# Two projections of a hybrid decoder: q and k computed channel by channel, and rotated by way of a DMA

## The chip, the cores and the metric

The kernel runs on one core of a Trainium2 chip. The metric is the device time of one execution in microseconds (us).

The engines are named as in the profile: PE multiplies matrices, PEld loads its weights, DVE, ACT and POOL work on vectors, SP issues most DMAs. Each engine works through its own queue in order. L537 is line 537 of the kernel; in the changed kernel the same line stands some ten to twenty lines further down.

## The reference

Two decoder layers on one sequence of 512 tokens, 1024 wide. Per layer, the normalised input is projected to ten groups of 512 columns, and four mixers work on them:

```
h    = rms_norm(x, g);  proj = h @ w_in           # 1024 -> 10 * 512
a_u, a_g, q, k, v, b_g, c_x, c_g, m_q, m_g = split(proj)
y_a  = s5_mixer(a_u)                              # state space, GLU
y_b  = rms_norm(diff_attention(rope(q), rope(k), v))
y_c  = rglru_mixer(c_x)                           # conv, gates, scan over time
y_m  = memory_attention(m_q, rms_norm(mem) @ w_mem_kv)
x   += concat(y_a*silu(a_g), y_b*silu(b_g), y_c*silu(c_g), y_m*silu(m_g)) @ w_out
```

q and k have 4 heads of 2 times 64 channels. `rope` rotates channels 0 to 15 of every 64: `x1*cos - x2*sin` and `x2*cos + x1*sin`, where x1 is channels 0 to 7, x2 is 8 to 15, and the angle depends on token and channel. Everything is float32.

## The kernel before, in words

**Split products.** Every weight comes by DMA in pieces of 128x1024 (`raw`). ACT casts a piece to `whi` (L166) and DVE subtracts to get the rest, `wlo` (L172). The input is split in the same way (hThi, hTlo). Each product is three matmuls: high by high, high by low, low by high.

**Two forms of a projection.** `tm_block` (L524) has the tokens as weights and gives token by channel, in four accumulators at once; its matmuls are L537. `cm_block` (L504) has the weight piece as weights and gives channel by token, in two accumulators, two calls for 512 columns; its matmuls are L517. There are four accumulators (`acc`) in PSUM in all.

**The order.** `ORDER` (L31) is the sequence of projections of each layer. `kv` stands for the memory's keys (`mk`, two calls of `cm_block`, 256 wide, four weight pieces) and values (`mv`, `tm_block` with two accumulators, four pieces). In layer 1 of before the sequence begins q, k, cx, v, kv.

**The streams.** Everything else runs beside the projections: attention (L610), the recurrent unit `lru` (L724, started when cx is finished), S5, the memory's norm. Each is a generator that is stepped at ticks, one per twelve matmuls of a projection. Attention has 16 items a layer (four token tiles by four heads): scores (L647, L648, L650) by PE, a maximum on DVE, exponentials on ACT (L658), a weighted difference on DVE, transposes on PE (L672), the product with v (L682), and two passes of ACT over it (L683, L685). A scheduler then orders the instructions of each engine by the program order and its own estimates, and where a buffer has to come free first, by that.

**lru.** Four channel blocks: a cast (L735), two products with small matrices `bd` (L740 to L742), two tanh on ACT (L743), a second tanh (L748), exponentials (L751), squares (L753), one root over 128x2048 (L756), and then on DVE a product with the root (`xc<-xc,li`) and a scan over time (L760). Only behind its last scan come its buffers free.

**Buffers.** `b8` tiles (128x2048) share 14 places. The result of mk and mv is a pair of them, `kv` high and low: ACT writes the high part (L796), DVE the low part (`kv<-acc,kv`), and with the latter the accumulator comes free.

**q and k.** Both are `tm_block`. `qk_evac` (L574) copies an accumulator to `qz` and rotates it by four DVE instructions; `flush_qk` (L591), called at each tick, transposes four 128x128 blocks on PE (L597) and copies them to `qT`, or splits them into the two `kT`.

Of the kernel before, what the change touches and what calls it, by code (L numbers as in the profile page):

```python
# [17 lines left out]
P = 128  # L18
# [9 lines left out]
ROPE_THETA = 500000.0  # L28


ORDER = ["q v k kv cx au cg bg mq ag mg gl oAM0 oAM1 oBC0 oBC1".split(),  # L31
         "q k cx v kv au mq bg mg ag cg gl oAM0 oAM1 oBC0 oBC1".split()]

C_ID, C_DM, C_IF, C_KEEP, C_CM, C_END = 0, 128, 144, 152, 152, 280

# [13 lines left out]


MEM_AHEAD = 2
BD_AHEAD = 3
S5P_AT = 2
D_MEM = (3, 2, 1)
D_S5 = (1, 1, 2, 2, 1, 2)
D_AT = 2


class Streams:
# [31 lines left out]
def tile_kernel(ctx: ExitStack, tc: tile.TileContext, A, out):  # L91
# [17 lines left out]
    def b8(shape, name, dtype=F32):  # L109
        return big.tile(shape, dtype, tag="b8", name=nm(name))  # L110
# [4 lines left out]
    def b2(shape, name, dtype=F32):  # L115
        return sm2.tile(shape, dtype, tag="b2", name=nm(name))
# [10 lines left out]
    def tp(shape=(P, 4, 128)):  # L127
        return ps.tile(list(shape), F32, tag="tp", bufs=2, name=nm("tp"))
# [51 lines left out]


    xr = A["x"].rearrange("o (t p) d -> p (o t) d", p=P)
    xd = ctx.enter_context(tc.tile_pool(name="xd", bufs=1, space=bass.MemoryType.DRAM)).tile([L, D], F32, tag="xd", name="xd")
    xdr = xd.rearrange("(t p) d -> p t d", p=P)
    xt = {}

# [32 lines left out]
    for l in range(DEPTH):  # L219
        for n in ORDER[l]:  # L220
            if n == "kv":
                for u in range(2):
                    add(l, "mk", u, cm_pieces(A["w_mem_kv"][l], 256 * u))
                add(l, "mv", 0, tm_pieces(A["w_mem_kv"][l], 512))
            elif n == "gl":
                w = A["s5_w_glu"][l].rearrange("(k p) (s c) -> p k s c", p=P, s=2)
                for u in range(2):
                    add(l, "gl", u, [w[:, 2 * i:2 * i + 2, :, 256 * u:256 * u + 256] for i in range(2)])
            elif n[0] == "o":
                ps_ = []  # L230
                for g in n[1:3]:
                    r0 = 512 * "ABCM".index(g)
                    ps_ += tm_pieces(w_out[l, r0:r0 + 512], 512 * int(n[3]))
                add(l, "o", n[1:], ps_)
            elif n in ("q", "k", "v", "au"):
                add(l, n, 0, tm_pieces(w_in[l], COL[n]))
            else:
                for u in range(2):
                    add(l, n, u, cm_pieces(w_in[l], COL[n] + 256 * u))
# [106 lines left out]
    def tt(o, a, b, op):  # L346
        V.tensor_tensor(out=o, in0=a, in1=b, op=op)  # L347
# [136 lines left out]
        V.tensor_scalar(out=cpos, in0=cpos, scalar1=4.0, scalar2=None, op0=ALU.mult)  # L484


    idb = const.tile([P, P], BF16, tag="idb", name="idb")
    cmb = const.tile([P, P], BF16, tag="cmb", name="cmb")
    V.tensor_copy(idb, ident)
# [81 lines left out]
        return ((lambda k, t: hi[k // 4][:, k % 4, t, :]), (lambda k, t: lo[k // 4][:, k % 4, t, :]))  # L571


    def qk_evac(dst):  # L574
        def f(t, a):
            z = b2([P, 8, 64], "qz")
            S.copy(z, a.rearrange("p (m d) -> p m d", d=64))
            z12 = z[:, :, 0:16].rearrange("p m (s f) -> p m s f", f=8)
            ca = rcos[:, t, :].unsqueeze(1).unsqueeze(1).to_broadcast([P, 8, 2, 8])
            sa = rsin[:, t, :].unsqueeze(1).unsqueeze(1).to_broadcast([P, 8, 2, 8])  # L580
            rab = b2([P, 2, 8, 2, 8], "rab")
            ra, rb = rab[:, 0], rab[:, 1]
            tt(ra, z12, ca, ALU.mult)
            tt(rb, z12, sa, ALU.mult)
            tt(z12[:, :, 0, :], ra[:, :, 0, :], rb[:, :, 1, :], ALU.subtract)
            tt(z12[:, :, 1, :], ra[:, :, 1, :], rb[:, :, 0, :], ALU.add)
            pend.append((dst, t, z, st.now))
        return f

    pend = []  # L590
    def flush_qk():  # L591

        while pend and st.now - pend[0][3] >= 2:
            dst, t, z, _ = pend.pop(0)
            pt = tp()
            for j in range(4):
                PE.transpose(pt[:, j, :], z[:, 2 * j:2 * j + 2, :].rearrange("p m d -> p (m d)"), ident)  # L597
            ts = slice(t * 128, (t + 1) * 128)
            if len(dst) == 1:
                S.copy(dst[0][:, :, ts], pt)  # L600
            else:

                for m in range(2):
                    own, oth = slice(m * 64, m * 64 + 64), slice(64 - m * 64, 128 - m * 64)
                    S.copy(dst[m][own, :, ts], pt[own])
                    tt(dst[m][oth, :, ts], pt[own], dst[m][own, :, ts], ALU.subtract)

    st.hook = flush_qk

    def attention(l, R):  # L610
        while pend or "par" in st.live:
            yield
        qT, kT, v = R["qT"][0], R["kT"], R["v"]
        o = qT
        R["o"] = o
        oss = const.tile([P, 16], F32, tag="oss", name=nm("oss"))
# [499 lines left out]
    def run(gen):  # L1116
        for _ in gen:
            st.tick()
# [36 lines left out]
    for pi, (l, n, u, ids) in enumerate(plan):  # L1155
# [6 lines left out]
        if any(p[0] == l and p[1] == "cx" for p in plan[pi:pi + BD_AHEAD]) and "bd" not in R:  # L1162
            lru_load(l, R)
        if n in ("q", "k"):
            R[n + "T"] = [b8([P, 4, L], "qT")] if n == "q" else [b8([P, 4, L], "kT", F32R) for _ in range(2)]
            run(tm_block(h_tm(), qk_evac(R[n + "T"]), ids))
        elif n == "v":
            vt = R["v"] = b8([P, NT, 512], "v")

# [78 lines left out]
        elif n == "gl":  # L1248
# [4 lines left out]
            for hf, pid in enumerate(ids):  # L1253
                whi, wlo = (w.rearrange("p (k s c) -> p k s c", k=2, s=2) for w in w_use(pid))
                for j in range(2):
# [13 lines left out]
                        ag = R["ag"][:, 2 * u + j, :]  # L1269
                        V.scalar_tensor_tensor(out=ag, in0=th, scalar=0.25, in1=ag, op0=ALU.mult, op1=ALU.mult)  # L1270
                    st.tick()
        if n in ("q", "k", "v") and all(a in R for a in ("qT", "kT", "v")):
            st.start("attn", attention(l, R))
        if n == "o":
            pair, half = u[:2], int(u[2])
# [99 lines left out]
```

## Time and profile before

| | us |
|---|---|
| median of three runs | 913.9 (913.62 to 914.91) |
| the profiled execution | 913.18 |
| its span | 911.4 |
| PE busy | 890.5 |
| DVE busy | 658.8 |
| ACT busy | 509.6 |

The busy time of PE comes from modelled ends: a matmul of 512 columns is shown as about 0.39 us long, and the next begins 0.23 us after it. So two starts are compared where a matmul's cost is wanted, and not the length of one.

### The profile page before, as it was taken

To read this page: it belongs to the slowest core of one execution; us is meant where nothing else is said; L and a number is where in the kernel's file an instruction comes from. 1 tells how busy PE (TensorE), PEld (TensorE's weight loads), DVE (VectorE), ACT (ScalarE), POOL (GpSimd) and SP (SyncE) were. 2 spreads that over 40 slices of the span, in tenths; PEclk is the share of its full clock that TensorE was granted. 3 is DMA by queue.
4 is the path that set the end of the run, shared out by engine and by line. 5 is a ranking of instruction groups with operands and counts; after the bars stand their busy time and mean duration, and the time that the engine had idled before them with its cause. 6 is when DMAs were issued, how large, how long until landed. Compare 5 with 4: busy or idle time off the path is not lost.

```text
span 911.4 us, 12490 instructions
## 1 busy us (share of the span) xinstructions
PE 890.5 (98%) x4542; PEld 748.9 (82%) x4542; DVE 658.8 (72%) x1315; ACT 509.6 (56%) x1031; POOL 42.1 (5%) x86
## 2 busy tenths in 40 slices
PE   8999999999999999999999999999999999999996
PEld 5788888978878888888888888898888888788885
DVE  6985888678999856983474667764899996666343
ACT  6764887985434265922554568766655344863133
POOL 1001000001110100000100000000101110000000
PEclk9999999999999999999999999999999999999999
DMA  5733432212222237432343332432112222152322
GB/s 185 196 118 102 140 93 70 70 47 72 75 70 61 75 104 205 135 111 93 127 140 92 93 93 70 137 95 70 51 47 83 63 74 93 47 185 98 108 72 93
DMA packets 80930, 90.07 MB, mean 99 GB/s; under 512 B 23778, under 2 KB 58211, under 8 KB 80868
## 3 DMA queue, kind: packets, MB, share of 16 engines
q1 hardware_dynamic: 77842, 85.72, 30.3%
q10 hardware_dynamic: 722, 2.36, 0.8%
q0 software_dynamic: 2304, 1.18, 0.5%
q8 instruction: 36, 0.59, 0.3%
q14 instruction: 26, 0.21, 0.1%
HBM read 84.40 MB, written 4.19 MB: 97 GB/s over the span
## 4 chain that ended last, share of the span: by engine, by line
PE 72%; DVE 18%; ACT 6%; issue 2%; DMA 1%; SPq 0%; DVEq 0%; ACTq 0%
PE acc L537 37%; PE acc L517 17%; PE acc L1261 5%; DVE wlo L172 2%; DVE u L347 2%; DVE xr L1046 2%; DVE wt L347 2%; PE ms L682 1%; DVE xr L347 1%; PE tp L312 1%; PE sc L810 1%; PE tp L1012 1%; PE sc L647 1%; PE sc L648 1%; ACT whi L166 1%
## 5 line engine op out<-in xcount | busy, mean ns | idle before, releaser
L172 DVE TENSOR_TENSOR wlo<-raw,whi 128x1024 fp32r<-128x1024 f32 x136 | 166.2, 1222 | 125.3 <-ACT whi L166 121.6
L166 ACT CAST whi<-raw 128x1024 fp32r<-128x1024 f32 x136 | 143.1, 1052 | 194.1 <-PE acc L537 120.1
L517 PE MATMUL acc<-hThi,whi 128*128 128x512 f32 x384 | 154.3, 402 | 0.0
L517 PE MATMUL acc<-hThi,wlo 128*128 128x512 f32 x384 | 151.1, 394 | 0.0
L517 PE MATMUL acc<-hTlo,whi 128*128 128x512 f32 x384 | 150.6, 392 | 0.0
L537 PE MATMUL acc<-whi,hThi 128*128 128x512 f32 x256 | 104.1, 407 | 1.0 <-ACT whi L166 1.0
L537 PE MATMUL acc<-wlo,hThi 128*128 128x512 f32 x256 | 100.7, 393 | 0.0
L537 PE MATMUL acc<-whi,hTlo 128*128 128x512 f32 x256 | 100.7, 394 | 0.0
L537 PE MATMUL acc<-wlo,mxh 128*128 128x512 f32 x256 | 100.2, 391 | 0.0
L537 PE MATMUL acc<-whi,mxh 128*128 128x512 f32 x256 | 100.1, 391 | 0.0
L537 PE MATMUL acc<-whi,mxl 128*128 128x512 f32 x256 | 100.1, 391 | 0.0
L517 PEld LDWEIGHTS acc<-hThi,wlo 128*128 128x128 f32 x384 | 72.2, 188 | 15.0
L517 PEld LDWEIGHTS acc<-hTlo,whi 128*128 128x128 f32 x384 | 72.4, 189 | 13.4
L517 PEld LDWEIGHTS acc<-hThi,whi 128*128 128x128 f32 x384 | 72.4, 189 | 13.0
L537 PEld LDWEIGHTS acc<-whi,hThi 128*128 128x128 f32 x256 | 56.3, 220 | 9.1 <-ACT whi L166 1.4
L537 PEld LDWEIGHTS acc<-whi,hTlo 128*128 128x128 f32 x256 | 56.1, 219 | 7.8 <-DVE hTlo L315 0.2
L537 PEld LDWEIGHTS acc<-wlo,hThi 128*128 128x128 f32 x256 | 56.4, 220 | 7.1
L537 PEld LDWEIGHTS acc<-whi,mxl 128*128 128x128 f32 x256 | 48.1, 188 | 9.8
L537 PEld LDWEIGHTS acc<-wlo,mxh 128*128 128x128 f32 x256 | 48.1, 188 | 9.7
L537 PEld LDWEIGHTS acc<-whi,mxh 128*128 128x128 f32 x256 | 48.1, 188 | 9.6
L982 POOL DMA_DIRECT2D MT<-kq x64 | 32.1, 509 | 490.7 <-DVE kq L347 339.4
L658 ACT ACTIVATE e<-sc,nmx 128x128 f32<-128x128 f32 (+3 forms) x64 | 33.1, 524 | 7.1 <-DVE nmx L654 5.8
(316 smaller groups left out, 1642.2 us busy)
## 6 DMA issues: line engine op xcount, KB each, us to landing
raw<-in_w_in_dram SPq DMA_DIRECT2D x80, 512.0 KB, 3.7
raw<-in_w_out_dram SPq DMA_DIRECT2D x32, 512.0 KB, 3.3
raw<-in_w_mem_kv_dram SPq DMA_DIRECT2D x16, 512.0 KB, 3.3
x<-in_x_dram SPq DMA_DIRECT2D x8, 512.0 KB, 4.7
raw<-in_s_w_glu_dram SPq DMA_DIRECT2D x16, 256.0 KB, 3.1
mt<-in_mem_dram SPq DMA_DIRECT2D x4, 512.0 KB
xd<-x SPq DMA_DIRECT2D x4, 512.0 KB, 4.0
x<-xd SPq DMA_DIRECT2D x4, 512.0 KB, 5.6
```

The costliest lines, as they stand in the source:

```text
L166: S.copy(hi, wbuf[j])
L172: V.tensor_tensor(out=lo, in0=raw, in1=hi, op=ALU.subtract)
L312: lastins["pe"] = PE.transpose(pt[:, k, :], h[:, kk * 128:(kk + 1) * 128], ident)
L347: V.tensor_tensor(out=o, in0=a, in1=b, op=op)
L517: PE.matmul(a[j][:, :ncol], w[:, kk, c], h(k), start=(hf == 0 and i == 0), stop=(hf == 1 and i == 3 * nh - 1))
L537: PE.matmul(a[t], h(k, t), w[:, kk, :], start=(p == 0 and kk == 0 and i == 0), stop=(p == np_ - 1 and kk == 1 and i == 2))
L647: PE.matmul(s[:, m, :M], qh[:, m, h, :], kT[m][:, h, :M], start=True, stop=False)
L648: PE.matmul(s[:, m, :M], ql[:, m, h, :], kT[m][:, h, :M], start=False, stop=False)
L658: S.activation(e[:, m, :N], s[:, m, :N], AF.Exp, bias=nmx[:, m:m + 1], scale=0.125, accum_out=sm[:, m:m + 1])
L982: G.dma_start(out=MT[g * 64 + 64 - n:g * 64 + 64, g, t], in_=kq[g * 64:g * 64 + n])
L1046: V.tensor_tensor_scan(out=xr_[i][:, j, :], data0=dec, data1=xr_[i][:, j, :], initial=0.0, op0=ALU.mult, op1=ALU.add)
L1261: PE.matmul(a, w[:, k, s, j * 128:(j + 1) * 128], h[:, 2 * hf + k, :], start=(hf == 0 and i == 0), stop=(hf == 1 and i == 5))
```

## The change

v comes first in both layers. q and k become `cm_block`, so their channels stand on the partitions, and attention takes its q straight from that tile (`qz`). To rotate, `rope` copies the 16 rows of every 64 that are to be rotated to a tile of their own with four POOL DMAs, computes with four DVE instructions, and writes them back with four DMAs. k is then split into the two `kT` with four ACT casts and four DVE subtractions of 64x1024. The cosines and sines that this needs, channel by token, are made once at the start: eight POOL copies, eight transposes on PE, four ACT copies; they are kept in DRAM for layer 1. Attention waits for both `rope` streams. `BD_AHEAD` goes from 3 to 1, which loads the small matrices of `lru` just before cx. By count, 64 transposes of q and k go and 8 come, ACT has 12 instructions fewer and DVE 56 fewer; the number of projection matmuls is the same.

```diff
@@ -28,8 +28,8 @@
 ROPE_THETA = 500000.0
 
-ORDER = ["q v k kv cx au cg bg mq ag mg gl oAM0 oAM1 oBC0 oBC1".split(),
-         "q k cx v kv au mq bg mg ag cg gl oAM0 oAM1 oBC0 oBC1".split()]
+ORDER = ["v q k kv cx au cg bg mq ag mg gl oAM0 oAM1 oBC0 oBC1".split(),
+         "v q k cx kv au mq bg mg ag cg gl oAM0 oAM1 oBC0 oBC1".split()]
 
 C_ID, C_DM, C_IF, C_KEEP, C_CM, C_END = 0, 128, 144, 152, 152, 280
 
@@ -49,11 +49,12 @@
 
 MEM_AHEAD = 2
-BD_AHEAD = 3
+BD_AHEAD = 1
 S5P_AT = 2
 D_MEM = (3, 2, 1)
 D_S5 = (1, 1, 2, 2, 1, 2)
 D_AT = 2
+D_ROPE = {"q": ((2, 2), (2, 2)), "k": ((4, 4), (2, 2))}
 
 class Streams:
@@ -232,7 +234,7 @@
                     r0 = 512 * "ABCM".index(g)
                     ps_ += tm_pieces(w_out[l, r0:r0 + 512], 512 * int(n[3]))
                 add(l, "o", n[1:], ps_)
-            elif n in ("q", "k", "v", "au"):
+            elif n in ("v", "au"):
                 add(l, n, 0, tm_pieces(w_in[l], COL[n]))
             else:
                 for u in range(2):
@@ -484,6 +486,23 @@
         V.tensor_scalar(out=cpos, in0=cpos, scalar1=4.0, scalar2=None, op0=ALU.mult)
 
+
+
+    rtab = [b2([P, L], f"rt{i}") for i in range(2)]
+    rtd = [dpool.tile([P, L], F32, tag=f"rtd{i}", name=f"rtd{i}") for i in range(2)]
+    for w, src in enumerate((rcos, rsin)):
+        rep_ = b2([P, NT, P], "rep")
+        for i in range(NT):
+            G.tensor_copy(rep_[:, i].rearrange("p (a f c) -> p a f c", a=4, c=4),
+                          src[:, i].unsqueeze(1).unsqueeze(3).to_broadcast([P, 4, 8, 4]))
+        pr = tp()
+        for i in range(NT):
+            PE.transpose(pr[:, i, :], rep_[:, i], ident)
+        pf = pr.rearrange("p i c -> p (i c)")
+        for s_ in range(2):
+            S.activation(rtab[w][s_ * 64:s_ * 64 + 64], pf[s_ * 64:s_ * 64 + 64], AF.Copy, scale=-1.0 if w == 1 and s_ == 1 else 1.0)
+        G.dma_start(out=rtd[w], in_=rtab[w])
+
     idb = const.tile([P, P], BF16, tag="idb", name="idb")
     cmb = const.tile([P, P], BF16, tag="cmb", name="cmb")
     V.tensor_copy(idb, ident)
@@ -571,46 +590,44 @@
         return ((lambda k, t: hi[k // 4][:, k % 4, t, :]), (lambda k, t: lo[k // 4][:, k % 4, t, :]))
 
-    def qk_evac(dst):
-        def f(t, a):
-            z = b2([P, 8, 64], "qz")
-            S.copy(z, a.rearrange("p (m d) -> p m d", d=64))
-            z12 = z[:, :, 0:16].rearrange("p m (s f) -> p m s f", f=8)
-            ca = rcos[:, t, :].unsqueeze(1).unsqueeze(1).to_broadcast([P, 8, 2, 8])
-            sa = rsin[:, t, :].unsqueeze(1).unsqueeze(1).to_broadcast([P, 8, 2, 8])
-            rab = b2([P, 2, 8, 2, 8], "rab")
-            ra, rb = rab[:, 0], rab[:, 1]
-            tt(ra, z12, ca, ALU.mult)
-            tt(rb, z12, sa, ALU.mult)
-            tt(z12[:, :, 0, :], ra[:, :, 0, :], rb[:, :, 1, :], ALU.subtract)
-            tt(z12[:, :, 1, :], ra[:, :, 1, :], rb[:, :, 0, :], ALU.add)
-            pend.append((dst, t, z, st.now))
-        return f
-
-    pend = []
-    def flush_qk():
-
-        while pend and st.now - pend[0][3] >= 2:
-            dst, t, z, _ = pend.pop(0)
-            pt = tp()
-            for j in range(4):
-                PE.transpose(pt[:, j, :], z[:, 2 * j:2 * j + 2, :].rearrange("p m d -> p (m d)"), ident)
-            ts = slice(t * 128, (t + 1) * 128)
-            if len(dst) == 1:
-                S.copy(dst[0][:, :, ts], pt)
-            else:
-
+    def rope(l, R, n):
+
+
+        z = R[n + "z"]
+        if l and n == "q":
+            rtab[:] = [b2([P, L], f"rt{i}") for i in range(2)]
+            for w in range(2):
+                G.dma_start(out=rtab[w], in_=rtd[w])
+        x1, x2 = b2([P, L], "rx"), b2([P, L], "ry")
+        rows = [(x1[s_ * 64 + m * 32:s_ * 64 + m * 32 + 32], z[m * 64 + s_ * 8:m * 64 + s_ * 8 + 8])
+                for s_ in range(2) for m in range(2)]
+        for x_, z_ in rows:
+            G.dma_start(out=x_, in_=z_)
+        yield D_ROPE[n][l][0]
+        co, si = rtab
+        for s_ in range(2):
+            to, fr = slice(s_ * 64, s_ * 64 + 64), slice(64 - s_ * 64, 128 - s_ * 64)
+            tt(x2[to], x1[fr], si[fr], ALU.mult)
+        tt(x1, x1, co, ALU.mult)
+        tt(x1, x1, x2, ALU.add)
+        for x_, z_ in rows:
+            G.dma_start(out=z_, in_=x_)
+        yield D_ROPE[n][l][1]
+        if n == "k":
+
+            kT = R["kT"] = [b8([P, 4, L], "kT", F32R) for _ in range(2)]
+            for h in range(0, 4, 2):
+                hs = slice(h, h + 2)
                 for m in range(2):
                     own, oth = slice(m * 64, m * 64 + 64), slice(64 - m * 64, 128 - m * 64)
-                    S.copy(dst[m][own, :, ts], pt[own])
-                    tt(dst[m][oth, :, ts], pt[own], dst[m][own, :, ts], ALU.subtract)
-
-    st.hook = flush_qk
+                    S.copy(kT[m][own, hs], z[own, hs])
+                    tt(kT[m][oth, hs], z[own, hs], kT[m][own, hs], ALU.subtract)
+                yield
 
     def attention(l, R):
-        while pend or "par" in st.live:
+        while any(n in st.live for n in ("par", "ropeq", "ropek")):
             yield
-        qT, kT, v = R["qT"][0], R["kT"], R["v"]
+        qT, kT, v = R["qz"], R["kT"], R["v"]
         o = qT
         R["o"] = o
         oss = const.tile([P, 16], F32, tag="oss", name=nm("oss"))
@@ -1162,8 +1179,15 @@
         if any(p[0] == l and p[1] == "cx" for p in plan[pi:pi + BD_AHEAD]) and "bd" not in R:
             lru_load(l, R)
         if n in ("q", "k"):
-            R[n + "T"] = [b8([P, 4, L], "qT")] if n == "q" else [b8([P, 4, L], "kT", F32R) for _ in range(2)]
-            run(tm_block(h_tm(), qk_evac(R[n + "T"]), ids))
+            if u == 0:
+                R[n + "z"] = b8([P, 4, L], n + "z")
+            zt = R[n + "z"]
+
+            def z_evac(j, a, u=u, zt=zt):
+                S.copy(zt[:, 2 * u + j, :], a)
+            run(cm_block(h_cm(), 8, z_evac, ids))
+            if u == 1:
+                st.start("rope" + n, rope(l, R, n))
         elif n == "v":
             vt = R["v"] = b8([P, NT, 512], "v")
 
@@ -1269,7 +1293,7 @@
                         ag = R["ag"][:, 2 * u + j, :]
                         V.scalar_tensor_tensor(out=ag, in0=th, scalar=0.25, in1=ag, op0=ALU.mult, op1=ALU.mult)
                     st.tick()
-        if n in ("q", "k", "v") and all(a in R for a in ("qT", "kT", "v")):
+        if n == "k" and u == 1:
             st.start("attn", attention(l, R))
         if n == "o":
             pair, half = u[:2], int(u[2])
```

The next rows are the order of DVE in layer 1 of before, at the end of `lru`. `wlo` is the low part of a weight piece, `mx` the maximum of an attention item.

```order
L347 TENSOR_TENSOR xc_4938<-xc_4938,li_5129 128x512 x2
L172 TENSOR_TENSOR wlo_5304<-raw_5192,whi_5302 128x1024
L760 SCALAR_TENSOR_TENSOR li_5129<-lr_5128,xc_4938 128x512 x2
L347 TENSOR_TENSOR xc_4938<-xc_4938,li_5129 128x512
L172 TENSOR_TENSOR wlo_5350<-raw_5264,whi_5348 128x1024
L652 TENSOR_REDUCE mx_5388<-sc_5371 128x2
L760 SCALAR_TENSOR_TENSOR li_5129<-lr_5128,xc_4938 128x512
L654 TENSOR_SCALAR nmx_5390<-mx_5388 128x2
L347 TENSOR_TENSOR xc_4938<-xc_4938,li_5129 128x512
L172 TENSOR_TENSOR wlo_5416<-raw_5306,whi_5414 128x1024
L760 SCALAR_TENSOR_TENSOR li_5129<-lr_5128,xc_4938 128x512
```

The same place on DVE in the changed kernel; L777 is the scan, `kv_5190` the low part of mk, and acc_5191 to acc_5369 are the four accumulators of mk.

```order
L771 SCALAR_TENSOR_TENSOR li_5236<-a_1032_5573,li_5236 128x512
L671 TENSOR_SCALAR nmx_5622<-mx_5620 128x2
L349 TENSOR_TENSOR xc_4953<-xc_4953,li_5236 128x512 x2
L777 SCALAR_TENSOR_TENSOR li_5236<-lr_5235,xc_4953 128x512 x2
L349 TENSOR_TENSOR xc_4953<-xc_4953,li_5236 128x512
...
L777 SCALAR_TENSOR_TENSOR li_5236<-lr_5235,xc_4953 128x512 x2
L349 TENSOR_TENSOR kv_5190<-acc_5191,kv_5189 128x256
L349 TENSOR_TENSOR kv_5190<-acc_5192,kv_5189 128x256
L349 TENSOR_TENSOR kv_5190<-acc_5368,kv_5189 128x256
L349 TENSOR_TENSOR kv_5190<-acc_5369,kv_5189 128x256
```

Before, weight pieces were split between the scans, and the accumulators of mk were emptied one by one later on. Now all four stand full until the last scan, and are emptied behind it in one go.

PE in the changed kernel, from the last matmul of mk to the first of mv (`acc_5522`); `sc` are scores of attention items.

```order
L536 MATMUL acc_5369<-mhi_5086,wlo_5279 128x256
L664 MATMUL sc_5461<-kT_5062,qh_5462 128x256
...
L664 MATMUL sc_5542<-kT_5062,qh_5462 128x256
...
L664 MATMUL sc_5613<-kT_5062,qh_5462 128x256
...
L664 MATMUL sc_5693<-kT_5062,qh_5462 128x256
...
L699 MATMUL ms_5718<-v_4532,pT_5636 128x128 x2
L556 MATMUL acc_5522<-whi_5370,mhi_5086 128x512
```

And PE in before, at the same step of the sequence.

```order
L517 MATMUL acc_5477<-mlo_5173,whi_5414 128x256
L517 MATMUL acc_5477<-mhi_5172,wlo_5416 128x256
L537 MATMUL acc_5604<-whi_5478,mhi_5172 128x512
L672 MATMUL tp_5581<-cst,e_5509 128x128
L682 MATMUL ms_5585<-v_5105,pT_5520 128x128
L537 MATMUL acc_5604<-wlo_5480,mhi_5172 128x512
```

In before mv followed mk at once. Now four attention items stand between the two, with no matmul of a projection among them.

PE early in layer 0 of the changed kernel, in the first projection (now v); `rep` is what POOL writes for the tables.

```order
L556 MATMUL acc_355<-whi_357,hThi_128 128x512
L500 MATMUL tp_301<-cst,rep_296 128x128 x4
L556 MATMUL acc_355<-wlo_359,hThi_128 128x512
L556 MATMUL acc_355<-whi_357,hTlo_130 128x512
L556 MATMUL acc_356<-whi_357,hThi_128 128x512
```

In before only projection matmuls stood here; the transposes of the tables are new on PE.

## Rows read from the trace of the kernel before

**Rows 1.** The page, parts 1 and 2: busy time, then forty slices of the span.
```profile
PE 890.5 (98%) x4542; PEld 748.9 (82%) x4542; DVE 658.8 (72%) x1315; ACT 509.6 (56%) x1031; POOL 42.1 (5%) x86
PE   8999999999999999999999999999999999999996
```
**Rows 2.** Busy time by window: stretch, its length, engines, granted clock, DMA share.
```profile
160.00:200.00 40.00, 40.00 (x210) 35.47 (x210) 26.18 (x42) 34.96 (x68) 0.00 (x0) 1.00 0.21 66
240.00:280.00 40.00, 38.53 (x213) 32.64 (x213) 39.33 (x71) 15.88 (x35) 8.01 (x16) 1.00 0.28 84
533.00:564.00 31.00, 31.00 (x150) 25.60 (x149) 21.22 (x29) 28.92 (x42) 0.00 (x0) 1.00 0.18 58
560.00:600.00 40.00, 39.06 (x243) 34.79 (x243) 33.17 (x63) 28.15 (x74) 0.00 (x0) 1.00 0.43 131
```
**Rows 3.** Timeline of PE around eight transposes of q: start, length, instruction.
```profile
42.43 0.39 PE L537 MATMUL acc<-whi,hTlo 128*128 128x512 f32 x1
42.66 1.03 PE L597 MATMUL tp<-cst,qz 128*128 128x128 f32 x8
43.45 0.47 PE L537 MATMUL acc<-whi,hThi 128*128 128x512 f32 x1
43.76 0.39 PE L537 MATMUL acc<-wlo,hThi 128*128 128x512 f32 x1
```
**Rows 4.** Groups by line and shape, PE: busy, mean ns, idle before, releasers.
```profile
L597 PE MATMUL tp<-cst,qz 128*128 128x128 f32 x64 | 8.9, 274 | 2.0 <-DVE tA L347 1.3 <-DVE kT L347 0.4 <-DVE rden L347 0.3
```
**Rows 5.** Timeline of PE early in layer 0.
```profile
29.51 0.39 PE L537 MATMUL acc<-whi,hThi 128*128 128x512 f32 x1
```
**Rows 6.** Timeline of DVE there: the last step of the cosines.
```profile
30.06 0.19 DVE L393 TENSOR_SCALAR cs<-cs 128x64 f32<-128x64 f32 x1
```
**Rows 7.** Groups by line and shape, POOL.
```profile
L1133 POOL DMA_DIRECT2D bd<-in_lru_w_a_dram x4 | 2.6, 663 | 0.0
...
L1129 POOL MEMSET bd<- 128x512 f32 x4 | 2.1, 526 | 212.8 <-issue 105.6 <-DVE sn L917 59.5 <-PE tp L891 26.6
```
**Rows 8.** Issues of DMAs: count, size, median us to landing.
```profile
bd<-in_lru_w_x_dram POOLq DMA_DIRECT2D x4, 64.0 KB, 3.2
```
**Rows 9.** Timeline of ACT in layer 1, from cx's last evacuation to the root.
```profile
534.29 0.58 ACT L1181 COPY cx<-acc 128x512 f32<-128x512 f32 x1
...
557.94 1.92 ACT L756 ACTIVATE li<-li 128x2048 f32<-128x2048 f32 x1
559.76 1.03 ACT L166 CAST whi<-raw 128x1024 fp32r<-128x1024 f32 x1
```
**Rows 10.** Timeline of DVE behind the root.
```profile
559.89 1.29 DVE L347 TENSOR_TENSOR xc<-xc,li 128x512 f32<-128x512 f32 x2 [2.54 <-ACT li L756]
...
562.24 2.33 DVE L760 TENSOR_TENSOR_SCAN li<-lr,xc 128x512 f32<-128x512 f32 x2
```
**Rows 11.** Timeline of ACT for one attention item.
```profile
575.50 0.36 ACT L658 ACTIVATE e<-sc,nmx 128x128 f32<-128x128 f32 x1
...
576.20 0.26 ACT L674 COPY pT<-tp 128x128 f32<-128x128 f32 x1
576.34 0.38 ACT L683 ACTIVATE qT<-ms,rc 128x128 f32<-128x128 f32 x1
...
576.95 0.39 ACT L796 CAST kv<-acc 128x256 fp32r<-128x256 f32 x1
```
**Rows 12.** Groups by line and shape, ACT.
```profile
L631 ACT CAST qh<-qT 64x512 fp32r<-64x512 f32 x16 | 9.9, 619 | 0.2
...
L605 ACT CAST kT<-tp 64x512 fp32r<-64x512 f32 x16 | 8.8, 581 | 2.8 <-PE tp L597 2.4
```
**Rows 13.** Timeline of PE in mk: one matmul, one attention item.
```profile
573.29 0.28 PE L517 MATMUL acc<-mhi,wlo 128*128 128x256 f32 x1
573.41 0.28 PE L647 MATMUL sc<-kT,qh 128*128 128x256 f32 x1
...
573.98 0.36 PE L517 MATMUL acc<-mhi,whi 128*128 128x256 f32 x1
```

More of the change, by code (lines that the diff above doesn't have):

```diff
@@ L182, in tile_kernel @@
     xr = A["x"].rearrange("o (t p) d -> p (o t) d", p=P)
-    xd = ctx.enter_context(tc.tile_pool(name="xd", bufs=1, space=bass.MemoryType.DRAM)).tile([L, D], F32, tag="xd", name="xd")
+    dpool = ctx.enter_context(tc.tile_pool(name="xd", bufs=1, space=bass.MemoryType.DRAM))
+    xd = dpool.tile([L, D], F32, tag="xd", name="xd")
     xdr = xd.rearrange("(t p) d -> p t d", p=P)
```

## The prediction

> **What bounds the kernel now.** I read the busy times first: PE is busy in 98% of the span, and in nearly every slice [rows 1]. So a change is worth what it takes from PE's queue, or what it makes PE wait. The second view is the busy time by window, for how near the other two engines are to their own limit: in 160 to 200 us ACT is busy 34.96 of 40 us, in 240 to 280 DVE 39.33 of 40, in 533 to 564 ACT 28.92 of 31 [rows 2]. In the last of these PE still never waits. The third view is the timeline, since a busy PE there is only two starts apart: matmuls of 512 columns begin 0.23 us apart [rows 3], of 256 columns 0.12 us [rows 13].
>
> All sums are made in the profiled execution (913.18 us, span 911.4); the median of the runs is 0.7 us above it, which I add at the end.
>
> **The transposes.** Eight of them stand between starts at 42.66 and 43.45, and the matmul behind them takes 0.31 us to its successor in place of 0.23 [rows 3]: 0.79 + 0.08 = 0.87 us, 0.109 each. 64 go and 8 come: -56 x 0.109 = -6.1 us. The projection matmuls stay in number and width, so they cost the same. PE waits 2.0 us in all in front of those transposes, 1.3 of it once, for DVE [rows 4]: -2.0. What is late next there is nothing on PE's path, since q's tile is needed only by attention.
> The Trainium skill, "TensorE: Matmul & The Clock Gate", Part 4 on the PE-mode transpose, gives about 275 ns for one transpose of 128x128 in a kernel's context. The trace agrees on the length (274 ns [rows 4]), but a length is not a cost here: by it 56 would be worth 15.4 us, an estimate that the starts contradict.
>
> **The tables at the start.** In the changed order the first transposes of the tables stand where PE is at about 29.6 us, one matmul after [rows 5]. The cosines end at 30.06 + 0.19 = 30.25 [rows 6], and then POOL makes four copies of 128x128. No such copy is in the trace; a memset of 128x512 takes 0.526 us [rows 7], so four copies take 0.5 us if they go by elements and 2.1 us if each costs as much as that memset. PE then waits until 30.8 to 32.4: 1.1 to 2.7 us, and I take 2.0. The second table's copies run under the six matmuls and the transposes behind the first; 0 to 0.4 us, taken as nothing. Everything behind the transposes in PE's queue is late by the same 2.0, since PE has no slack.
>
> **The rotation by DMA.** POOL issues four copies out and four back, 0.66 us each [rows 7], of 64 KB; the nearest transfer of this size lands after 3.2 us [rows 8]. So 2.6 + 3.2 = 5.8 us from the first issue to the last landing, against two ticks of 24 matmuls, 24 x 0.23 = 5.5 us. DVE may wait 0.3 us for each trip, with a weight piece queued behind. Between that and twice as much (a first landing that takes as long as the issues) it is 0 to 1.5 us on DVE; PE gets nothing of it as long as the pieces are made several us ahead. I take 0. POOL itself has 5% of the span to do [rows 1]. ACT and DVE instructions that go or come are hidden under PE, except in the two places that follow.
>
> **Layer 1 from cx to mv.** This is the term that decides. Before, v came between cx and kv: 96 x 0.23 = 22 us of PE work beside which `lru` ran. Now mk follows cx at once. In the changed order DVE empties the four accumulators of mk only behind the last scan of `lru`, and mv, which needs these accumulators, stands behind that on PE. So I compare when that scan ends with how much PE has to do until then, both from the end of cx (T0).
> ACT: in before the root over 128x2048 ended 557.94 + 1.92 = 559.86, and cx's last copy began at 534.29 [rows 9]: 25.6 us, with ACT 93% busy. In the changed order, the same stretch of ACT's queue has in addition two casts of weights (2 x 1.03 [rows 9] = 2.1), four casts of k of 64x1024 (512 elements take 0.58 [rows 12], 1024 in a weight's cast 1.03: between 2.3 and 4.6, I take 4.1), four casts of mk (4 x 0.39 [rows 11] = 1.6), the exponentials of six items (575.50 to 576.20 is 0.70 an item [rows 11], two of them wider by about 0.2: 4.6), six copies of transposed items (0.14 to 0.3: 1.2), four pairs behind the product with v (576.34 to 576.95, 0.61 each [rows 11]: 2.4), and four casts of q (4 x 0.62 [rows 12] = 2.5). Together 18.5, so 44.1 us to the end of the root if ACT waits no more than before.
> DVE behind the root: two products 1.2 us to the next start and two scans 2.33 [rows 10], so four of each 7.1, small instructions of attention about 0.9, and the first emptied accumulator 0.4. mv begins at T0 + 52.5.
> PE until then: 96 matmuls of 256 columns x 0.12 = 11.5; 24 products of `lru` x 0.23 = 5.5; scores of eight items, 573.41 to 573.98 [rows 13], x 0.57 = 4.6; 26 transposes and 8 products with v x 0.11 = 3.7. Together 25.3. So PE waits 27 us if ACT waits no more than it did.
> It will wait more: each item goes from PE to DVE to ACT and back, and one tile of scores is there at a time. At the 87% of 160 to 200 us in place of 93%, 44.1 becomes 47.2 and the wait 30; reckoned as work that ACT fills to 87% it is 50.7 and 34. I take 32. The low end is 25 (k's casts at 0.58), the high end 46: the 70% share of ACT in 560 to 600 [rows 2], where attention, mk and weights ran together, makes 44.1 into 63.
>
> **Attention later in layer 0.** It starts when k is rotated, so some six items more fall into S5's stretch, with about 1.7 us of DVE each, 10 us, where DVE is busy 39.33 of 40 and PE loses 1.5 already [rows 2]. Weight pieces are made up to some pieces ahead, so most is swallowed: 0 to 5, I take 1.5.
>
> **Small waits in kv.** In 560 to 600 PE lost 0.94 us [rows 2] by attention beside mk; these go into the long wait: -1.
>
> **Sum.** -6.1 - 2.0 + 2.0 + 32 + 1.5 - 1 = +26.4: 939.6 in the profiled execution, 940 by the median.
>
> **Rivals.**
> 1. The other side, faster: mk's accumulators come free in time. The point from which it decides is whether the last scan ends before PE has done its 25.3 us behind cx. Then only -6.1 - 2.0 + 2.0 + 0.5 - 0 is left, 908. For it speaks that PE never waited in 533 to 564 [rows 2]; against it that the same chain took 25.6 us to the root alone, without attention, and 7 us of products and scans come behind it. Chance 0.06, with a spread of 905 to 911.
> 2. Only `lru`'s own chain counts, since attention's and k's ACT work (18.5 us) comes earlier or later than the order suggests, as it would if the rotations landed late: 25.6 + 8.4 - 25.3 leaves a wait of 9, so 940 - 23 = 917. Chance 0.08, spread 914 to 924.
> 3. S5's stretch in layer 0 is the second loss: DVE is full there, and 10 us more work is 10 us more time beyond what is swallowed, on top of the forecast: 948. For it speaks the 39.33 of 40 [rows 2], against it that other stretches around have room. Chance 0.12.
> 4. PE's clock. The granted clock is 1.00 in all windows read, also in 533 to 564 [rows 2], but in before PE is never thin for long. If PE, doing 25 us of work in nearly 60, came down to the lower level of 1.2 GHz, its work would be hidden in the wait, but scores in the chain of an item and the first matmuls behind would take twice their 0.23: some ten matmuls and four items, 3 to 5 us more, 944. Chance 0.12.
> The Trainium skill, "TensorE: Matmul & The Clock Gate", Part 1 on the HAM clock gate, says that an array that was idle falls to 1.2 GHz and has to be warmed by work; no stretch of before shows it on a long wait.
>
> The forecast itself, a long wait in layer 1 and the rest small, has 0.62: 930 to 953. The 80% range is 924 to 954: it leaves out rival 1, most of rival 2, and the far end of the waits. What a measurement of this kernel can tell from no change is about 0.2%, 1.8 us: faster 0.06, the same 0.03 (the low end of rival 2), slower 0.91.
>
> **What would show it.** In the profile after: two or three slices of PE well below 9 in the middle of the span, and there ACT above 85%; the longest wait of PE by far in front of the first matmul of mv, put down to a DVE `kv` instruction, with all scans before it; the root ending 44 to 51 us after cx's last copy. Small: a wait of 1 to 3 us at about 30 us for POOL's `rep`, none for q's transposes. I am wrong if PE stays full in layer 1 (rival 1), if the root comes some 26 us after cx (rival 2), or if PE thins out at 200 to 320 us (rival 3).

## The result: 4% slower, and the profile after

The changed kernel takes 949.7 us (948.2 to 951.2) against 913.8; the ratio is 1.0389 (95% interval 1.0373 to 1.0405). The forecast was 940, between 924 and 954. The profiled execution took 949.12 us with a span of 947.3, 35.9 us more than before.

Parts 1 and 2 of the page, as in [rows 1], with the granted clock:

```profile
PE 897.8 (95%) x4486; PEld 750.6 (79%) x4486; DVE 656.3 (69%) x1259; ACT 506.4 (53%) x1019; POOL 64.7 (7%) x130
...
PE   7999799999999999999999969389999999999997
...
PEclk9999999999999999999999989589999999999999
```

Only POOL has clearly more to do, 64.7 us in place of 42.1, and PE is shown 7.3 us busier with 56 instructions fewer, in part because its matmuls are longer where the clock is low. But PE has a hole in slices 24 to 27, at 545 to 639 us, a small one in the fifth slice, and the clock falls in the large one. The windows (columns as in [rows 2]):

```profile
80.00:120.00 40.00, 34.91 (x199) 29.95 (x198) 26.29 (x33) 21.99 (x32) 7.73 (x14) 0.97 0.49 141
...
560.00:600.00 40.00, 27.76 (x168) 24.15 (x168) 28.26 (x50) 33.30 (x76) 0.00 (x0) 0.82 0.16 53
600.00:640.00 40.00, 28.39 (x114) 24.28 (x115) 24.41 (x44) 20.93 (x42) 0.00 (x0) 0.71 0.23 66
```

Then the chain in the hole, which answers to [rows 9, 10]. ACT: cx's last copy (L1205), two casts of k, a gap, and the root (L773).

```profile
557.90 0.58 ACT L1205 COPY cx<-acc 128x512 f32<-128x512 f32 x1
...
559.06 1.98 ACT L623 CAST kT<-kz 64x1024 fp32r<-64x1024 f32 x2
...
568.28 0.58 ACT L316 CAST mhi<-tp 128x512 fp32r<-128x512 f32 x1 [4.13 <-PE tp L314]
...
609.41 1.91 ACT L773 ACTIVATE li<-li 128x2048 f32<-128x2048 f32 x1
```

DVE behind the root: the last scans (L777), and mk's first low part.

```profile
617.31 2.33 DVE L777 TENSOR_TENSOR_SCAN li<-lr,xc 128x512 f32<-128x512 f32 x2
619.67 0.42 DVE L349 TENSOR_TENSOR kv<-acc,kv 128x256 fp32r<-128x256 f32 x1
```

PE: the first score, held for kT, the score with the longest wait, and the first matmul of mv.

```profile
562.03 0.58 PE L664 MATMUL sc<-kT,qh 128*128 128x256 f32 x1 [4.94 <-DVE kT L349]
565.20 0.58 PE L664 MATMUL sc<-kT,qh 128*128 128x256 f32 x1 [2.37 <-DVE kT L349]
...
613.71 0.58 PE L664 MATMUL sc<-kT,qh 128*128 128x256 f32 x1 [5.16 <-ACT e L675]
...
620.15 0.80 PE L556 MATMUL acc<-whi,mhi 128*128 128x512 f32 x1 [1.17 <-DVE kv L349]
```

From cx's last copy to mv are 62.25 us, for which PE had 25.3 us of work by the prediction's count: 37 us are lost. PE's waits in this stretch add up to 26.6 us; the rest is inside what is shown as busy, in part matmuls at the lower clock. The label "1.17 <-DVE kv" names only the end of it. The rest of the hole is booked on attention's scores, which stand in PE's queue ahead of mv, so the list of waits alone would have blamed attention.

### The profile page after: what moved, and what is told of

The parts are those of the page before. It is cut to its first block, busy times and chain, and to the rows that moved or that the text cites. A ratio compares the mean times of both kernels' runs of the same rounds, so it can differ in the third digit from the quotient of the medians.

```text
span 947.3 us, 12364 instructions
## 1 busy us (share of the span) xinstructions
PE 897.8 (95%) x4486; PEld 750.6 (79%) x4486; DVE 656.3 (69%) x1259; ACT 506.4 (53%) x1019; POOL 64.7 (7%) x130
## 4 chain that ended last, share of the span: by engine, by line
PE 70%; DVE 18%; ACT 7%; DMA 3%; issue 2%; POOL 0%; SPq 0%; DVEq 0%; ACTq 0%
PE acc L556 27%; PE acc L536 26%; PE acc L1285 5%; DVE wlo L173 3%; DVE u L349 2%; DVE xr L1063 2%; DVE wt L349 1%; DVE xr L349 1%; PE tp L314 1%; ACT whi L167 1%; PE ms L699 1%; PE sc L827 1%; DVE li L777 1%; PE tp L852 1%; PE sc L664 1%
## 5 line engine op out<-in xcount | busy, mean ns | idle before, releaser
L536 PE MATMUL acc<-hThi,whi 128*128 128x512 f32 x512 | 204.0, 398 | 0.0
L536 PE MATMUL acc<-hThi,wlo 128*128 128x512 f32 x512 | 202.5, 395 | 0.0
L536 PE MATMUL acc<-hTlo,whi 128*128 128x512 f32 x512 | 202.0, 395 | 0.0
L536 PEld LDWEIGHTS acc<-hThi,wlo 128*128 128x128 f32 x512 | 96.6, 189 | 19.6 <-DVE wlo L173 0.2
L536 PEld LDWEIGHTS acc<-hTlo,whi 128*128 128x128 f32 x512 | 96.7, 189 | 18.4
L536 PEld LDWEIGHTS acc<-hThi,whi 128*128 128x128 f32 x512 | 96.7, 189 | 18.0
L556 PE MATMUL acc<-whi,hThi 128*128 128x512 f32 x128 | 53.3, 416 | 0.8 <-ACT whi L167 0.8
L556 PE MATMUL acc<-wlo,hThi 128*128 128x512 f32 x128 | 52.0, 406 | 0.0
L556 PE MATMUL acc<-whi,hTlo 128*128 128x512 f32 x128 | 50.7, 398 | 0.0
L664 PE MATMUL sc<-kT,qh 128*128 128x256 f32 (+2 forms) x64 | 23.1, 366 | 22.4 <-DVE kT L349 10.4
L669 DVE TENSOR_REDUCE mx<-sc 128x2 f32<-128x256 f32 (+3 forms) x32 | 26.2, 819 | 13.0 <-PE sc L667 12.9
```

The source lines that it names most:

```text
L536: PE.matmul(a[j][:, :ncol], w[:, kk, c], h(k), start=(hf == 0 and i == 0), stop=(hf == 1 and i == 3 * nh - 1))
L556: PE.matmul(a[t], h(k, t), w[:, kk, :], start=(p == 0 and kk == 0 and i == 0), stop=(p == np_ - 1 and kk == 1 and i == 2))
L664: PE.matmul(s[:, m, :M], qh[:, m, h, :], kT[m][:, h, :M], start=True, stop=False)
L669: V.tensor_reduce(out=mx, in_=s[:, :, :N], op=ALU.max, axis=AX.X)
```

## The experiments

Times are medians; each ratio is against runs of the kernel before on the same chip (914.2 to 914.6 us).

**Who holds mk.** Three cures, each for one reading of the hole.

v back between cx and kv in layer 1 (attention starts when k and v are both there):

```diff
-         "v q k cx kv au mq bg mg ag cg gl oAM0 oAM1 oBC0 oBC1".split()]
+         "q k cx v kv au mq bg mg ag cg gl oAM0 oAM1 oBC0 oBC1".split()]
```

> Changed kernel with layer 1's sequence as before (q, k, cx, v, kv), so v's 22 us of matmuls stand between cx and mk; attention starts behind v. Theory A (mk's four accumulators are held until the recurrent unit's last scan, and PE has only 25 us of work until then): v covers most of the 37 us lost there, so 949.7 - 32 to - 40 = 910 to 918, and PE has no window under 36 of 40 us in the middle of the span. Rival B (the rotation by DMA comes late, and PE stands at scores that wait for kT: 10.4 us in the waits): attention begins later too, but the first scores still stand ahead of work; some 8 us stay, 920 to 926. Rival C (only the fall of the clock to 0.5 costs): the clock stays at 1.0 only if the thin stretch goes, so the same as A and no test of C.

Measured 922.8 us, 1.0097 (1.0075 to 1.0119): 27 us back, less than A said and inside B's range. The hole is gone (PE is busy 39.02 us in 560 to 600), and the one wait for kT that is left, 3.1 us, is layer 0's. So what is left above A's number is a new loss, not B's: q is now the first projection of layer 1, by `cm_block`, which needs the hidden state of all four token tiles from its first matmul on, where v by `tm_block` starts with one tile. PE at the layer's boundary:

```profile
472.46 1.29 PE L314 MATMUL tp<-cst,h 128*128 128x128 f32 x8 [2.04 <-DVE h L304]
477.23 1.94 PE L314 MATMUL tp<-cst,h 128*128 128x128 f32 x8 [3.48 <-DVE h L304]
```

The recurrent unit started behind mv in layer 1:

```diff
-            if u == 1:
+            if u == 1 and l == 0:
                 st.start("lru", lru(l, R))
...
+            if l == 1:
+                st.start("lru", lru(l, R))
```

> Changed kernel, sequence unchanged, but in layer 1 the recurrent unit starts behind mv instead of behind cx, so its buffers are not in use when mk is emptied. Theory A: mk is emptied as it is done and PE goes on: the waits from 591 to 620 us go (about 26 us with the slow clock), the 9 us at 557 to 567 for kT stay: 949.7 - 26 = 924, at most 918 to 930. Rival B (the rotation is what is late, the rest follows from it): less than 10 us come back, 940 or more.

Measured 925.9 us, 1.0127 (1.0112 to 1.0142): 23.8 back. B falls, which allowed less than 10: the wait for kT is still there in full, 10.4 us in the list of waits as before the cure.

A low part of its own for mk:

```diff
-    sm2 = ctx.enter_context(tc.tile_pool(name="sm2", bufs=10))
+    sm2 = ctx.enter_context(tc.tile_pool(name="sm2", bufs=8))
...
-                R["kv"] = [b8([P, 2048], "kv", F32R) for _ in range(2)]
+                R["kv"] = [b8([P, 2048], "kv", F32R), kmlo]
...
+            R["vml"] = vml_ = b8([P, 1024], "vml", F32R)
```

> Changed kernel, sequence and starts unchanged; mk's low part has a 4 KB tile of its own, mv's low part a buffer taken at mv, and the pool of small tiles has 8 in place of 10 places to make room. Only the buffer that mk waits for is taken away, ACT's work stays. Theory A with the buffer as the cause: mv starts some 35 us after cx in place of 62, and its 11 us and au's first matmuls cover the rest: 20 to 30 us come back, 920 to 930. Rival D (not the buffer but ACT's load: 44 us of work against 25 us of PE's, whoever holds what): weight pieces come no faster, 5 us or less come back, 944 to 950. Two small tiles fewer may cost 0 to 3 us elsewhere.

Measured 929.7 us, 1.0165 (1.0148 to 1.0182): 20.0 back, with ACT's work and the sequence untouched. DVE in this kernel (L778 is the scan):

```profile
576.18 0.42 DVE L349 TENSOR_TENSOR kmlo<-acc,kv 128x256 fp32r<-128x256 f32 x1
...
594.51 0.42 DVE L349 TENSOR_TENSOR kmlo<-acc,kv 128x256 fp32r<-128x256 f32 x1 [0.29 <-ACT kv L814]
...
607.96 2.33 DVE L778 TENSOR_TENSOR_SCAN li<-lr,xc 128x512 f32<-128x512 f32 x2
...
617.22 1.22 DVE L778 TENSOR_TENSOR_SCAN li<-lr,xc 128x512 f32<-128x512 f32 x1
```

The emptying of mk begins 32 us ahead of the first scan and ends 13 us ahead of it. So it was the buffer, one of the 14 large places that only the last scan gives back, and not ACT's load as such (D falls).

**kv ahead of cx in layer 1:** the sequence is `v q k kv cx au`.

> Changed kernel with layer 1's sequence v, q, k, kv, cx, au, as in layer 0. Theory A: kv meets only attention's first items, the recurrent unit runs under au's 22 us; 949.7 - 30 to - 38 = 912 to 920, with a wait for kT in layer 1 like the 3 us of layer 0. Rival B: two such waits of 5 us, 918 to 925. Rival D (ACT's load): the same work of ACT is spread over 22 us more of PE's, so about as A.

Measured 921.0 us, 1.0067 (1.0051 to 1.0084), with two waits for kT of 3.1 us on average: 1 us above A's range, within B's, D not told apart.

**What the rotation costs by itself.** The kernel before in the same sequence:

```diff
-ORDER = ["q v k kv cx au cg bg mq ag mg gl oAM0 oAM1 oBC0 oBC1".split(),
-         "q k cx v kv au mq bg mg ag cg gl oAM0 oAM1 oBC0 oBC1".split()]
+ORDER = ["v q k kv cx au cg bg mq ag mg gl oAM0 oAM1 oBC0 oBC1".split(),
+         "v q k kv cx au mq bg mg ag cg gl oAM0 oAM1 oBC0 oBC1".split()]
```

> Kernel before with both layers in the sequence v, q, k, kv, cx, au, its q and k still by tokens with transposes. Against the changed kernel in the same sequence (kv before cx, 921.0) it gives the price of the rotation by DMA alone. Theory: 921.0 is 7 us above before because attention begins some 20 us after k's last matmul (two trips and the split of k) and PE stands at its first scores; without the trips no such wait, 911 to 914, so the rotation costs 7 to 10 us net of the 6 us of transposes it saves. Rival (layer 1's new sequence is itself what costs): 918 to 922.

Measured 914.0 us, 0.9994 (0.9985 to 1.0002). So the sequence as a whole costs nothing, and projection by channel with rotation by DMA costs 7.0 us net (6.7 by the two ratios, as the runs were on different chips), although it takes some 6 us of transposes from PE. The 7 us hold everything else that the change brings, the tables at the start and `BD_AHEAD` among it; `BD_AHEAD` was not tried alone.

The kernel before with only layer 0's sequence changed to v, q, k:

> Kernel before with layer 0's sequence v, q, k, kv, cx in place of q, v, k, kv, cx, nothing else. It puts a number on the waits of q's transposes apart from the rotation: PE stood 1.95 us more than its work at 36.8 to 39.8 us while DVE had the tables to make. Theory: that wait goes, since v needs no transposes: 913.9 - 2 = 911 to 913. Rival: moving q later only moves its DVE work into k and kv, no gain: 913.5 to 915.

Measured 912.8 us, 0.9981 (0.9972 to 0.9990): the wait of q's transposes is worth 1.7 us, and v first is enough to get it. It is the fastest kernel of this study; since the run above has the same layer 0 and gains nothing, its new sequence in layer 1 seems to cost about 1 us.

**Where these 7 us are.** The trips made longer in the sequence with kv before cx: `"k": ((6, 6), (6, 6))`.

> Changed kernel with layer 1's sequence v, q, k, kv, cx and, for k in both layers, 6 ticks in place of 4 and 2 for each trip of the rotation by DMA (a tick is 1.4 us in mk). Compared with the run with kv before cx (921.0). Theory: DVE stood 2.6 us in front of the copied rows in layer 0, weight pieces came late by that, and so did kT: PE lost 5.6 us there and some 5 in layer 1; with longer trips half of it comes back, 914 to 918. Rival: kT's place in ACT's queue is what is late, whatever the trips: 920 to 922, or later still since attention starts later.

Measured 926.3 us, 1.0129 (1.0113 to 1.0144). The theory failed as a cure: the waits for kT shrank to 2.2 us, though the rival said that they would not, but attention came later and met S5 in layer 1. PE there:

```profile
690.34 0.77 PE L664 MATMUL sc<-kT,qh 128*128 128x512 f32 x1 [4.17 <-DVE u L349]
697.82 0.80 PE L664 MATMUL sc<-kT,qh 128*128 128x512 f32 x1 [5.20 <-ACT e L675]
```

k before q, so that k's trips run under q (`"v k q kv cx au"` in both layers; here and in all runs with k before q, attention is started behind q):

> Both layers in the sequence v, k, q, kv, cx; k's trips of 3 ticks run under q's 22 us of matmuls, its split is done before attention begins; q's trips have 6 ticks under mk. Theory (kv away from the recurrent unit, and kT early, each worth its own wait): no wait for kT is left, 921.0 - 5.6 - 5 = 908 to 913, faster than before. Rival (the 7 us that remain above before with kv before cx are due to attention later in the S5 stretch, not to kT): 917 to 921.

Measured 921.8 us, 1.0079 (1.0061 to 1.0097): 0.8 us above the rival's range. No wait for kT is left; in its place scores wait 6.6 us for q's cast (`qh`), and 2.9 us for S5's DVE work, so the rival's cause is only a part of it.

The last sequence in layer 0, and in layer 1 `v k q cx kv au`:

> As the last one in layer 0; layer 1 has v, k, q, cx, kv: kT is early, but mk still follows cx at once. It tells the two waits of layer 1 apart. Theory: they add up; kT's 9 us (and layer 0's 5) go, the wait for the buffer behind the last scan stays, 26 to 30 us: 934 to 940. Rival (the late kT delays attention's first items, which fill ACT, so the long wait is its consequence): with kT early the long wait shrinks too, 915 to 928.

Measured 940.5 us, 1.0283 (1.0268 to 1.0298): 9.1 back, 0.5 us short of the theory's range, and the long wait stands. No score waits for kT any more, but of layer 0's 5 us only 2.4 came back (PE is busy 37.27 us in 80 to 120). DVE in layer 1:

```profile
611.23 1.21 DVE L777 TENSOR_TENSOR_SCAN li<-lr,xc 128x512 f32<-128x512 f32 x1
612.48 1.42 DVE L349 TENSOR_TENSOR kv<-acc,kv 128x256 fp32r<-128x256 f32 x4
```

A block of matmuls over the trips: `v k q bg kv cx au` in both layers.

> Changed kernel in the sequence v, k, q, bg, kv, cx in both layers: k's trips run under q, q's trips (3 ticks each) under bg's 22 us, so that both are done when attention begins, and au with S5 comes a block later. Theory (the rotation costs only by its latency): with a block of matmuls over it, no wait at first scores and no attention in S5's full stretch; the transposes' 6 us are left as a gain, 906 to 911. Rival (attention and kv together fill ACT and DVE whenever they start): 914 to 921.

Measured 934.0 us, 1.0208 (1.0194 to 1.0222): wrong, and not by the rival either. Windows of this kernel:

```profile
80.00:120.00 40.00, 39.80 (x223) 34.50 (x222) 26.21 (x32) 22.81 (x30) 4.37 (x8) 1.00 0.46 120
320.00:360.00 40.00, 33.95 (x168) 27.99 (x167) 27.18 (x55) 26.12 (x49) 0.00 (x0) 0.87 0.28 93
780.00:820.00 40.00, 26.29 (x137) 21.07 (x136) 27.54 (x54) 22.90 (x43) 4.00 (x8) 0.83 0.18 68
```

PE is full where the trips are, as it should be. But PE now loses 6 and 14 us at S5's and the memory attention's end. I read this as bg having been their cover; no run tests that apart. bg between cx and au instead:

> Changed kernel in the sequence v, k, q, kv, cx, bg, au in both layers: as the run with k before q (921.8), but bg stands in front of au, so S5 starts 22 us later and attention is further on by then; q's trips still run under mk. It tells the two parts of what remained there apart: the waits at the first scores (about 4 us in each layer) and attention in S5's stretch (some 7 us at 680 to 700 us). Theory: the second part goes, 912 to 917; the first stays. Rival (S5's stretch is as full without attention): 920 to 923.

Measured 938.9 us, 1.0278 (1.0262 to 1.0294): wrong in the same way, 5.3 us alone for the memory attention's `me`, and the first waits stay too. So no run shows one place where the 7 us are: each cure of one wait brought another.

**Both cures of layer 1 at once:** k early, and the recurrent unit behind mv.

> The two single cures together, layer 1 in the sequence v, k, q, cx, kv as in the run with k early and kv last (940.5), and its recurrent unit started behind mv as in the run with the unit late (925.9). Theory (two waits of layer 1 that add up: kT's 9 us and the buffer's 24): 949.7 - 9.1 - 23.8 = 917, between 914 and 920. Rival (the late kT and the held buffer are one loss seen twice): no better than the better of the two, 924 to 927. In neither is it under before, since attention still begins later.

Measured 915.1 us, 1.0003 (0.9994 to 1.0012). The two waits add up (917 expected by addition), and the changed kernel so mended is level with before. So the 7.0 us above are the price of the rotation in that one sequence, not a fixed one. Its window in place of the hole:

```profile
560.00:600.00 40.00, 39.85 (x233) 35.87 (x233) 29.57 (x63) 29.18 (x82) 0.00 (x0) 1.00 0.40 124
```

A larger pool for the large buffers was not tried; for the 4 KB of mk's own low part room had to be taken from the small tiles.

## Why the prediction was right, point by point

**The hole in layer 1: the mechanism right, the size 5 us short.** It was to be 32 us with an end at 46, and is 37. ACT's work was sized well: it was busy 42.73 us from cx's last copy to the root, against 42.3 forecast (93% of 25.6, and the 18.5 added), as this window shows:

```profile
557.90:611.30 53.40, 33.31 (x190) 28.43 (x190) 35.02 (x65) 42.73 (x92) 0.00 (x0) 0.76 0.15 50
```

But that is 80% of the stretch, not 87%, and the root came after 53.4 us, not the 44 to 51 foretold. 4.1 us of ACT's idle time is the gap in front of `mhi` (L316) in ACT's rows: PE stood at scores for kT, and the transposes that ACT waited for stood behind them. The term "ACT waits no more than before" was made from stretches in which no queue stood still. kT alone does not explain the share: in the run with k early and kv last no score waits for it, k's casts lie outside the stretch, and the root comes after 48.0 us with ACT still at 82%. Its mv begins 56.8 us behind cx's copy, 5.4 us less than here:

```profile
556.14:604.13 47.99, 33.09 (x176) 26.05 (x174) 30.64 (x61) 39.19 (x87) 0.00 (x0) 0.79 0.17 55
...
612.96 0.80 PE L556 MATMUL acc<-whi,mhi 128*128 128x512 f32 x1
```

Two of the signs named ahead did not come: ACT is not above 85% there, and PE's longest wait is not in front of mv (1.17 us) but in front of a score (5.16). That mv starts only behind all scans did come.

**The rotation taken at 0: the step that failed.** The argument was that DVE is late by little and PE gets nothing. The first trip of k in layer 0 took from 88.25 to 94.63, 6.4 us for 5.8 foretold. The rows of POOL and of DVE:

```profile
88.25 2.16 POOL L605 DMA_DIRECT2D rx<-kz  x4 [11.22 <-ACT kz L1187]
...
99.25 2.18 POOL L614 DMA_DIRECT2D kz<-rx  x4 [5.45 <-DVE rx L349]
```

```profile
94.63 1.40 DVE L349 TENSOR_TENSOR ry<-rx,rt 64x512 f32<-64x512 f32 x2 [2.58 <-DMA rx<-kz]
```

The ticks were miscounted without harm: this trip has four of them, in mk, 48 matmuls of 256 columns or 5.8 us, near the 5.5 taken. But DVE came to the rows 3.8 us after the first issue and stood 2.6 us. PE lost more than that, in front of a score and before that for weights:

```profile
107.59 0.50 PE L556 MATMUL acc<-whi,mhi 128*128 128x512 f32 x1 [1.26 <-ACT whi L167]
108.86 0.50 PE L556 MATMUL acc<-wlo,mhi 128*128 128x512 f32 x1 [0.76 <-DVE wlo L173]
...
116.81 0.39 PE L664 MATMUL sc<-kT,qh 128*128 128x256 f32 x1 [3.08 <-DVE kT L349]
```

That is 4.6 us more lost in 80 to 120 than in before:

```profile
80.00:120.00 40.00, 39.49 (x247) 33.87 (x245) 32.33 (x70) 29.92 (x68) 3.06 (x5) 1.00 0.40 125
```

PE was to get nothing "as long as the pieces are made several us ahead", and this is what did not hold. ACT's rows:

```profile
94.41 1.05 ACT L167 CAST whi<-raw 128x1024 fp32r<-128x1024 f32 x1 [3.07 <-DMA raw<-in_w_mem_kv_dram]
...
106.50 1.04 ACT L167 CAST whi<-raw 128x1024 fp32r<-128x1024 f32 x1 [3.84 <-DMA raw<-in_w_mem_kv_dram]
...
112.59 1.05 ACT L167 CAST whi<-raw 128x1024 fp32r<-128x1024 f32 x1 [3.20 <-DMA raw<-in_w_in_dram]
113.55 0.58 ACT L813 CAST kv<-acc 128x512 fp32r<-128x512 f32 x1
114.02 1.99 ACT L623 CAST kT<-kz 64x1024 fp32r<-64x1024 f32 x2
```

From 91 to 113 us ACT waited five times for a weight piece, 12.5 us in all; in 80 to 120 of before it did so once, for 0.6 us. kT's casts stand in ACT's queue behind the last of these pieces. The rows copied back had landed by 107.7 (the last was issued by 101.4, and no copy of k in this stretch took over 6.3 us), so I read kT as late by its place behind the weights more than by DVE's 2.6 us.

Why the weights came late stays open. In 80 to 120 us they landed 4.1 us after their issue (median, at most 5.5), against 3.5 (at most 4.4) in before, which speaks for the rotation's transfers beside them. But with k before q they landed after 3.6 (at most 3.8), and ACT still waited 4.4 us for one. So there is a second reading, that kv without attention beside it runs faster than its weights come. The run with attention in kv (bg in front) has no such wait, but it moved more than that.

**S5 in layer 0 (1.5):** nothing in 240 to 280 us, where it was looked for; PE is busy there for longer than before [rows 2]. But in 160 to 200 us, where before lost nothing, a transpose of attention waits 1.84 us for S5's copies on ACT (`U`). So about the size came, on another engine and earlier.

```profile
160.00:200.00 40.00, 38.16 (x189) 33.13 (x188) 29.37 (x46) 33.50 (x67) 0.00 (x0) 1.00 0.18 57
...
199.93 0.33 PE L689 MATMUL tp<-cst,e 128*128 128x128 f32 x1 [1.84 <-ACT U L952]
...
240.00:280.00 40.00, 39.69 (x245) 33.97 (x244) 39.26 (x77) 24.26 (x57) 5.77 (x12) 1.00 0.22 69
```

Rival 3 is out for the change as it stands, though the runs with longer trips and with k before q ran into S5's stretch of layer 1.

**The tables (2.0):** 0.86. Four copies of the cosines took 1.05 us, near the low bound.

```profile
31.44 1.05 POOL L496 COPY rep<-cs 128x128 f32<-128x128 f32 x4 [27.97 <-DVE pl L479]
32.43 2.03 POOL L496 COPY rep<-sn 128x128 f32<-128x128 f32 x4
```

**The transposes (-6.1) and their waits (-2.0):** the waits were tried in layer 0 (-1.7). The transposes were not tried alone; nothing in the runs speaks against 0.109 us each.

**The clock (rival 4):** it did fall. Windows of the changed kernel in layer 0, inside the hole, and behind it:

```profile
118.00:121.20 3.20, 3.20 (x9) 2.42 (x9) 3.17 (x4) 1.46 (x2) 0.00 (x0) 0.50 0.15 16
...
605.00:610.00 5.00, 2.28 (x11) 1.65 (x10) 1.87 (x5) 2.36 (x4) 0.00 (x0) 0.50 0.00 0
620.00:625.00 5.00, 4.85 (x15) 3.93 (x16) 4.47 (x11) 2.50 (x5) 0.00 (x0) 0.69 0.00 0
```

The lower level of 1.2 GHz is granted after the 3.1 us wait at 116.81 and in the hole. By these rows it costs 5 x 0.31 = 1.6 us behind mv's start and 3.2 x 0.50 = 1.6 us in layer 0, an estimate; what it costs inside the hole no run separates. So it is a rider on the losses, not a rival to them. The Trainium skill, "TensorE: Matmul & The Clock Gate", Part 1 on the HAM clock gate, says that an idle array falls to 1.2 GHz: the trace agrees, with 0.50.

**Together** (against the profiled execution of before): 37 in layer 1, 4.6 in layer 0, 1.6 and 1.6 for the clock, 0.9 for the tables and 1.8 in 160 to 200 us, less 6.1, 2.0 and 1.0, and less 1.2 that PE gained in 240 to 280, make 37.2; measured are 35.9. Some of these terms were never tried alone, so that the sum comes this near is partly chance. What the page itself shows is that PE's idle time rose by 28.6 us and its busy time by 7.3. The forecast of 940 missed by 10 us mainly because the hole was 5 us larger and the rotation, with its clock, cost 6 in layer 0 in place of 0.

## What to carry to other kernels

Read in the order of each engine which instruction gives a buffer back, and what stands between that and the next block on the busiest engine: mk, emptied only after a long chain on two other engines, cost 20 us by its buffer alone, and 24 with the unit that held it out of the way. Look also at what stands ahead of a late result in its own queue: kT waited behind weights that had not come. Moving a block of matmuls over a new wait may uncover an old one, as happened with bg. No run here made the transfer pay, though it takes some 6 us of work from the bound engine: without cover PE waited for kT, and with cover it waited elsewhere.

## What the runs showed of the hardware that I had not expected

PE's granted clock went to 0.50 about a microsecond after a single wait of 3.1 us in layer 0 had ended, while waits of 1.3 and 0.8 us at 106 to 109 us, and that of 1.3 us in before [rows 4], left it at 1.00. Copies of 64 KB between 8-partition rows and a 128-partition tile landed after 3.1 to 4.3 us (medians of eight), up to a third more than the 3.2 taken from [rows 8]; but the loads from which that was taken landed after 4.5 us in this kernel, so the copies are not slower than other transfers of their size here. POOL's copy of 128x128 took 0.26 us for one table and 0.51 for the other.
